# Feed-forward norms: the second token tile's four folds and the last early lo parts queue behind the first tile's normalisation, and the early hi parts form one run

## The chip, the cores and the metric

The kernel runs on one core of a Trainium2 chip. The metric is device time in microseconds of one execution; the time before is the median of three runs. One further execution was profiled, and all rows below are from it. Four engines matter: the tensor engine (PE), the vector engine (VectorE, shown as DVE), the scalar engine (ScalarE, shown as ACT) and the SP queue that issues the weight loads. Each executes its own list of instructions strictly in the order in which they stand, and waits on semaphores for the others.

## The reference, cut to what matters

```python
def _swiglu(x, w1, w3, w2):
    return (silu(x @ w1) * (x @ w3)) @ w2

for l in range(2):                     # x: 256 tokens x 1024
    x = _layernorm(ALPHA * x + 0.5 * _swiglu(x, w1[l,0], w3[l,0], w2[l,0]), g[l,0], b[l,0])
    x = _layernorm(ALPHA * x + Mixer(x), g[l,1], b[l,1])
    x = _layernorm(ALPHA * x + 0.5 * _swiglu(x, w1[l,1], w3[l,1], w2[l,1]), g[l,2], b[l,2])
```

Mixer(x) starts with a projection of x (its `val` section) and ends with `m @ w_out`. There are two layers with three layer norms each: four behind a feed-forward part (the last of them makes the output) and two behind a mixer.

## The kernel before, in words

**Tiles.** The 256 tokens are two token tiles of 128 (t = 0, 1; `xtok_143` and `xtok_144` in the lists below). The 1024 columns are two halves (c or h = 0, 1).

**Weights.** `stream` (L154) loads 128x2048 float32 of weights with one DMA into a buffer `raw` (there are four), ScalarE writes a rounded copy, the hi part (L173), and VectorE the rest, the lo part (L175). Matmuls use (hi, x hi), (lo, x hi), (hi, x lo). Parts named `whi`/`wlo` take slots of a pool of eight; at a transition `gemm_b2` borrows room from another pool for the first six 512-wide pieces, named `lhi`/`llo` here: the early parts (`lent`, L327: both halves of the first load and one half of the second).

**End of a feed-forward part** (`ffn`, from L654). The last product, h @ w2, is made with a seven-product scheme; its products lie in banks S[1] to S[7]. VectorE folds them into x: `ln.more` (L475 to L480) is one 128x512 fold. There are two folds for tile 0 and four for tile 1: `more(1, 0, S[7])` at L667, and those with v, u and S[7] at L674 to L676. Then for each tile and half the held weight pieces give the rest of the product into one more bank (`rows_p`, L681: 24 matmuls), and `ln.part` adds that bank to x (L487) and takes statistics of the half (L492). `ln.finish` (L496) aggregates them (L499), computes the reciprocal square root in eight steps on one column (`rsqrt`, L187 to L193), and normalises two halves (L503). This is called the first (t = 0) or the second (t = 1) normalisation below.

**The way into the next stage.** The tensor engine transposes the normalised halves (`turn`, L547): those of tile 0 stand in its list among the products of tile 1, and those of tile 1 among the first products of the next stage. ScalarE applies gain and bias to a transposed half (`xf`, L553) and writes x hi (L180), VectorE x lo (L181). The next stage begins with `gemm_b2` (L321): tile 0 with all four loads, then tile 1 with the same parts.

**What sets the order.** The tensor engine's list is the order of the code, with `turn` placed by a count of beats. On the other engines a scheduler orders instructions by priority and by when it expects inputs. Two means override it: `soon()` raises the priority of ScalarE's and VectorE's work on the transposes, and `behind(ins)` queues an instruction behind `ins` on that engine. Early hi parts are queued behind `latest[0]`, the last x hi of the stage before. The lo parts have `after` (L328): in the second load the early half has none of its own, so it falls back on `latest[1]`, and the other half is queued behind `norm.ends[0]`, the first normalisation.

Of the kernel before, what the change touches and what calls it, by code (L numbers as in the profile page):

```python
# [16 lines left out]
AF = mybir.ActivationFunctionType  # L17
ALU = mybir.AluOpType
# [23 lines left out]
HC = CH // 2  # L42
# [15 lines left out]
def trunk(ctx, tc, x, xT, w13a, w13b, w2s, w2p, wb, wqk, wa, wbr, wo, gateb, sgug, sgub, sguwT, sgubias, lam, diffg,  # L58
# [88 lines left out]

    latest, added, emptied, silu, turned_by = [None, None], [None], [None], [None], [None]

# [4 lines left out]
    def stream(src, width=CH, sub=HC, lent=(), after=(None, None)):  # L154
# [7 lines left out]
        for o in range(0, width, HC):  # L162
# [7 lines left out]
            for p, (h, w) in zip(range(0, HC, sub), at):  # L170
                r = raw[:, o + p : o + p + sub]
                with behind(latest[0]):
                    A.activation(h, r, AF.Copy)  # L173
                with behind(after[o // HC] or latest[1]):
                    V.tensor_tensor(out=w, in0=r, in1=h.bitcast(F32), op=ALU.subtract)  # L175
# [145 lines left out]
    def gemm_b2(srcs, xh, xl, done, norm=None):  # L321
# [4 lines left out]
        if norm:  # L326
            lent = [(0, 1), (0,), (), ()]  # L327
            after[1:3] = (None, norm.ends[0]), (norm.ends[0], norm.ends[0])  # L328
        ps = [[bank() for _ in range(2)] for _ in range(NT)]
        got = [[None] * 4 for _ in range(2)]  # L330
        for t in range(NT):
            for c in range(2):
# [3 lines left out]
                for m in range(2):  # L336
                    n = 2 * c + m
                    if t == 0:
                        got[m][2 * c : 2 * c + 2] = stream(srcs[m][:, c * CH : (c + 1) * CH], sub=512, lent=lent[n],
                                                           after=after[n])  # L340
                    for i in range(2 * c, 2 * c + 2):
                        rows_b(ps[t][m], t, 2 * i, got[m][i], xh, xl, KT)
            with behind(latest[0] if t == 0 else None):
                done(t, ps[t])
# [221 lines left out]
    def ffn(l, f, i, norm, last=False):  # L566
# [99 lines left out]
        ln.more(0, 0, S[1], ALU.add, ln.scale)  # L666
        ln.more(1, 0, S[7], ALU.subtract, ln.scale)  # L667
        V.tensor_tensor(out=u, in0=u, in1=S[1], op=ALU.add)
        V.tensor_tensor(out=v, in0=S[5], in1=u, op=ALU.subtract)
        ln.more(0, 1, v, ALU.add, ln.scale)  # L670
        for m in range(HELD // 2):
            q = PQ[len(PQ) - HELD + 2 * m :][:2]
            held.update({(k, 1): w for k, w in zip(q, stream(w2p[l, f, len(PQ) - HELD // 2 + m]))})
        ln.more(1, 1, v, ALU.add, ln.scale)  # L674
        ln.more(1, 0, u, ALU.add)
        ln.more(1, 1, S[7], ALU.add)  # L676
        for t in range(NT):
            for c in range(2):
                for ps, o, n in ends[t, c]:
                    for q in PQ[-HELD:]:  # L680
                        rows_p(ps, t, q, held[q, c], hh, hl, o, n, stop=q == PQ[-1])  # L681
                    for o in ((0, 256) if last and (t, c) == (1, 1) else (0,)):
                        ln.part(t, c * 512 + o, ps[:, o : o + 256] if o or last and (t, c) == (1, 1) else ps, 1.0)
            ln.finish(t, ((2, 1.5), (2, 1))[t])
        return ln.close()

# [319 lines left out]
```

## Time and profile before

| | us |
|---|---|
| median of three runs (1225.89 to 1226.11) | 1226.04 |
| the profiled execution | 1224.48 |
| its span, first to last instruction | 1222.7 |
| PE busy | 1209.9 (99%) |
| DVE busy | 954.5 (78%) |
| ACT busy | 813.1 (66%) |

1.78 us of the profiled execution lie around its span. A row of the timeline is: start in us, duration in us (of the whole group where it ends in x2 or more), engine, line, operation, output <- input, shapes, count, and in brackets the idle time of the engine just before it with what ended it. Overlapping durations are normal: a next instruction can begin before the one ahead has ended.

### The profile page before, as it was taken

How to read it: one execution, taken by the hardware profiler on the slowest of the kernel's cores; microseconds unless marked ns; L12 is line 12 of the kernel's file. 1: busy time of each engine (PE TensorE's matmuls, PEld its weight loads, DVE VectorE, ACT ScalarE, POOL GpSimd, SP SyncE). 2: the span in 40 equal slices, each digit the busy share in tenths (PEclk: the TensorE clock that was granted, in tenths of full speed). 3: DMA queues.
4: the chain of work that ended last, by engine and by line, in shares of the span. 5: the costliest groups of instructions: out<-in, count | busy, mean ns of one | idle time of the engine just before them, and what ended most of it. 6: DMA issues, size and time to landing. Idle time of an engine off the chain costs nothing.

```text
span 1222.7 us, 16592 instructions
## 1 busy us (share of the span) xinstructions
PE 1209.9 (99%) x6033; PEld 1018.2 (83%) x6033; DVE 954.5 (78%) x1540; ACT 813.1 (66%) x1328; POOL 88.0 (7%) x184
## 2 busy tenths in 40 slices
PE   9999999999999999999999999999999999999998
PEld 8888878888888888888788888788888888888886
DVE  6658998886587985679985679978856879747797
ACT  7677666679665665775666776666795655667761
POOL 0100000244100000000000000002430000000000
PEclk9999999999999999999999999999999999999999
DMA  8975665654754657675667655756446446577551
GB/s 318 333 245 180 220 225 202 218 168 167 248 172 166 219 181 254 194 202 207 238 192 251 197 175 206 268 189 211 161 171 240 172 163 250 175 238 206 182 202 49
DMA packets 82339, 252.29 MB, mean 206 GB/s; under 512 B 47520, under 2 KB 48592, under 8 KB 55632
## 3 DMA queue, kind: packets, MB, share of 16 engines
q1 hardware_dynamic: 78288, 238.31, 58.0%
q0 software_dynamic: 3536, 12.13, 2.9%
q8 instruction: 47, 0.77, 0.2%
q10 hardware_dynamic: 432, 0.79, 0.2%
q14 instruction: 36, 0.29, 0.1%
HBM read 235.47 MB, written 1.05 MB: 193 GB/s over the span
## 4 chain that ended last, share of the span: by engine, by line
PE 89%; DVE 7%; issue 2%; ACT 1%; DMA 0%; DVEq 0%; ACTq 0%
PE bank L215 34%; PE sbank L215 21%; PE bank L227 17%; PE bank L234 9%; PE sbank L227 2%; PE bank L386 2%; DVE wlo L175 2%; DVE slo L299 1%; PE sbank L736 1%; PE sbank L547 1%; PE sbank L234 1%; DVE llo L175 1%; PE sbank L785 1%; PE sbank L866 1%; DVE raw L310 1%
## 5 line engine op out<-in xcount | busy, mean ns | idle before, releaser
L175 DVE TENSOR_TENSOR wlo<-raw,whi 128x1024 fp32r<-128x1024 f32 (+1 forms) x402 | 441.3, 1116 | 158.5 <-ACT whi L173 118.2
L173 ACT ACTIVATE whi<-raw 128x1024 fp32r<-128x1024 f32 (+1 forms) x402 | 378.7, 966 | 181.3 <-PE bank L215 62.1
L215 PE MATMUL bank<-whi,x 128*128 128x512 f32 x840 | 264.6, 390 | 0.0
L215 PEld LDWEIGHTS bank<-whi,x 128*128 128x128 f32 x840 | 157.7, 188 | 32.6
L215 PE MATMUL bank<-wlo,x 128*128 128x512 f32 x420 | 163.5, 389 | 0.0
L215 PE MATMUL sbank<-whi,x 128*128 128x512 f32 x512 | 158.9, 389 | 0.0
L227 PE MATMUL bank<-x,whi 128*128 128x512 f32 x640 | 158.3, 395 | 0.0
L227 PEld LDWEIGHTS bank<-x,whi 128*128 128x128 f32 x640 | 116.5, 188 | 26.0 <-issue 2.7
L215 PEld LDWEIGHTS sbank<-whi,x 128*128 128x128 f32 x512 | 96.1, 188 | 19.9
L297 ACT ACTIVATE shi<-raw 128x1024 fp32r<-128x1024 f32 (+1 forms) x80 | 73.4, 946 | 51.8 <-DVE raw L312 26.7
L215 PE MATMUL sbank<-wlo,x 128*128 128x512 f32 x256 | 99.6, 389 | 0.0
L299 DVE TENSOR_TENSOR slo<-raw,shi 128x1024 fp32r<-128x1024 f32 (+1 forms) x80 | 85.2, 1087 | 14.4 <-ACT shi L297 13.6
L215 PEld LDWEIGHTS bank<-wlo,x 128*128 128x128 f32 x420 | 78.9, 188 | 16.0
L234 PE MATMUL bank<-x,wlo 128*128 128x256 f32 x640 | 85.8, 285 | 0.0
L234 PEld LDWEIGHTS bank<-x,wlo 128*128 128x128 f32 x640 | 81.5, 191 | 2.3
L553 ACT ACTIVATE xf<-sbank,ln_b,ln_g 128x128 f32<-128x128 f32 x80 | 30.0, 456 | 45.8 <-PE sbank L547 45.8
L235 ACT ACTIVATE r<-bank 128x256 f32<-128x256 f32 x112 | 41.8, 379 | 27.6 <-PE bank L234 27.6
L215 PEld LDWEIGHTS sbank<-wlo,x 128*128 128x128 f32 x256 | 48.0, 188 | 10.1
L215 PE MATMUL sbank<-whi,hhi 128*128 128x512 f32 x144 | 56.3, 391 | 0.0
L215 PE MATMUL sbank<-whi,hlo 128*128 128x512 f32 x144 | 56.1, 389 | 0.0
L215 PE MATMUL sbank<-wlo,hhi 128*128 128x512 f32 x144 | 56.0, 389 | 0.0
L446 POOL DMA_DIRECT2D bc<-in_lng x6 | 3.2, 530 | 712.1 <-DVE bc L445 712.1
(233 smaller groups left out, 1977.0 us busy)
## 6 DMA issues: line engine op xcount, KB each, us to landing
raw<-in_w13b SPq DMA_DIRECT2D x76, 1024.0 KB, 5.4
raw<-in_w2p SPq DMA_DIRECT2D x24, 1024.0 KB, 4.9
raw<-in_wa SPq DMA_DIRECT2D x24, 1024.0 KB, 5.3
raw<-in_w2s SPq DMA_DIRECT2D x20, 1024.0 KB, 4.8
raw<-in_wb SPq DMA_DIRECT2D x16, 1024.0 KB, 4.9
raw<-in_wqk SPq DMA_DIRECT2D x16, 1024.0 KB, 4.8
raw<-in_wbr SPq DMA_DIRECT2D x16, 1024.0 KB, 4.8
raw<-in_w13a SPq DMA_DIRECT2D x8, 1024.0 KB, 4.8
```

What stands on the lines that cost most here:

```text
L173: A.activation(h, r, AF.Copy)
L175: V.tensor_tensor(out=w, in0=r, in1=h.bitcast(F32), op=ALU.subtract)
L215: PE.matmul(ps, xx, w, start=start and n == 0, stop=stop and n == 2)
L227: PE.matmul(b[-1], hi[:, k * P : (k + 1) * P], xc(k), start=k == 0, stop=False)
L234: PE.matmul(b[n][:, :T], lo[:, k * P : (k + 1) * P], xc(k)[:, :T], start=False, stop=k == KT - 1)
L235: emptied[0] = A.activation(r[:, s], b[n][:, T:], AF.Copy, scale=scale).ins
L297: A.activation(h, r, AF.Copy)
L299: V.tensor_tensor(out=w, in0=r, in1=h.bitcast(F32), op=ALU.subtract)
L310: V.tensor_tensor(out=raw[:, :1024], in0=raw[:, :1024], in1=raw[:, 512:1536], op=ALU.add)
L386: PE.matmul(ps[t][m], x[:, j, o + t * P : o + (t + 1) * P], y, start=k0 + j == 0 and o == 0 and y is hi, stop=k0 + j == KT - 1 and y is lo)
L547: PE.transpose(b[:, k * P : (k + 1) * P], self.y[t][:, h * 512 + k * P : h * 512 + (k + 1) * P], ident)
L553: A.activation(xf[:, s], b[:, s], AF.Identity, scale=self.gT[:, f], bias=self.bT[:, f])
```

## The change

- `ffn`: the four folds of tile 1 are no longer issued with those of tile 0; they stand behind `ln.finish(0)`, queued behind the second half of the first normalisation (`ln.ends[0]`). In the last feed-forward part there is no such instruction (`ends[0]` stays None), and only their place in the code moves.
- `gemm_b2`: `after[1:3]` now queues both halves of the second load, and so the last two early lo parts, behind the first normalisation. This is so behind the mixers' norms too.
- `stream`: a hi part that isn't early is queued behind the last early hi part given so far (`early[0]`) instead of behind `latest[0]`; the early ones stand as one run.

```diff
-    latest, added, emptied, silu, turned_by = [None, None], [None], [None], [None], [None]
+    latest, added, emptied, silu, turned_by, early = [None, None], [None], [None], [None], [None], [None]
...
-                with behind(latest[0]):
-                    A.activation(h, r, AF.Copy)
+                with behind(latest[0] if o // HC in lent else early[0] or latest[0]):
+                    copied = A.activation(h, r, AF.Copy)
+                if o // HC in lent:
+                    early[0] = copied.ins
...
-            after[1:3] = (None, norm.ends[0]), (norm.ends[0], norm.ends[0])
+            after[1:3] = [(norm.ends[0], norm.ends[0])] * 2
...
+            early[0] = None
             with behind(latest[0] if t == 0 else None):
                 done(t, ps[t])
...
         ln.more(0, 0, S[1], ALU.add, ln.scale)
-        ln.more(1, 0, S[7], ALU.subtract, ln.scale)
...
-        ln.more(1, 1, v, ALU.add, ln.scale)
-        ln.more(1, 0, u, ALU.add)
-        ln.more(1, 1, S[7], ALU.add)
...
             ln.finish(t, ((2, 1.5), (2, 1))[t])
+            if t == 0:
+                with behind(ln.ends[0]):
+                    ln.more(1, 0, S[7], ALU.subtract, ln.scale)
+                    ln.more(1, 0, u, ALU.add)
+                    ln.more(1, 1, v, ALU.add, ln.scale)
+                    ln.more(1, 1, S[7], ALU.add)
```

In the changed file the lines stand a little lower: L175 becomes L177, L181 L183, L480 L483, L487 L490, L492 L495, L503 L506, L547 L550, L553 L556. The lists of the tensor engine, GpSimd and SP are the same as before, row for row. VectorE's and ScalarE's differ at the norms: in the same way behind the first three feed-forward parts, in another behind the two mixers, and in the last feed-forward part only tile 1's folds move, between tile 0's two sums.

VectorE ahead of the first normalisation of the first norm (L503), before: three of tile 1's folds, the first sum of tile 0 (`bank_1213`) and what follows.

```order
L480 SCALAR_TENSOR_TENSOR xtok_144<-xtok_144,v_1492 128x512
L478 TENSOR_TENSOR xtok_144<-xtok_144,u_1491 128x512
L478 TENSOR_TENSOR xtok_144<-xtok_144,sbank_1210 128x512
L487 TENSOR_TENSOR xtok_143<-xtok_143,bank_1213 128x512
L175 TENSOR_TENSOR llo_1720<-raw_1716,lhi_1718 128x512
L492 BN_STATS st_1199<-xtok_143 128x6
L487 TENSOR_TENSOR xtok_143<-xtok_143,sbank_1209 128x512
```

The same engine in the change, from the first normalisation (L506) on.

```order
L506 TENSOR_SCALAR xtok_143<-xtok_143,mv_1590,nwy_1605 128x512 x2
L483 SCALAR_TENSOR_TENSOR xtok_144<-xtok_144,sbank_1210 128x512
L483 SCALAR_TENSOR_TENSOR xtok_144<-xtok_144,v_1492 128x512
L481 TENSOR_TENSOR xtok_144<-xtok_144,u_1491 128x512
L481 TENSOR_TENSOR xtok_144<-xtok_144,sbank_1210 128x512
L490 TENSOR_TENSOR xtok_144<-xtok_144,sbank_1211 128x512
L177 TENSOR_TENSOR llo_1750<-raw_1746,lhi_1748 128x512
L495 BN_STATS st_1200<-xtok_144 128x6
L177 TENSOR_TENSOR llo_1751<-raw_1746,lhi_1749 128x512
L183 TENSOR_TENSOR x_1207<-xf_1651,x_1207 128x4x128
```

Eight rows that stood ahead of the first normalisation now stand behind it: the four folds, the two early lo parts `llo_1750` and `llo_1751`, and tile 1's first sum (`sbank_1211`) with its statistics, which need the folds.

VectorE ahead of the second normalisation of the same norm, before: from the reciprocal square root on, with x lo of the second half (`x_1208`).

```order
L181 TENSOR_TENSOR x_1208<-xf_1681,x_1208 128x4x128
L193 TENSOR_SCALAR nwy_1701<-nwa_1700,nwy_1697 128x1
L175 TENSOR_TENSOR wlo_1815<-raw_1812,whi_1814 128x512
L192 TENSOR_SCALAR nwa_1704<-nwy_1701,ve_1692 128x1
L175 TENSOR_TENSOR wlo_1815<-raw_1812,whi_1814 128x512
L193 TENSOR_SCALAR nwy_1705<-nwa_1704,nwy_1701 128x1
L175 TENSOR_TENSOR wlo_1821<-raw_1812,whi_1820 128x512
L503 TENSOR_SCALAR xtok_144<-xtok_144,mv_1690,nwy_1705 128x512 x2
L175 TENSOR_TENSOR wlo_1821<-raw_1812,whi_1820 128x512
```

The same place in the change.

```order
L177 TENSOR_TENSOR wlo_1783<-raw_1774,whi_1782 128x512
L194 TENSOR_SCALAR nwa_1696<-yi_1693,ve_1692 128x1
L177 TENSOR_TENSOR wlo_1815<-raw_1812,whi_1814 128x512
L195 TENSOR_SCALAR nwy_1697<-nwa_1696,yi_1693 128x1
L177 TENSOR_TENSOR wlo_1815<-raw_1812,whi_1814 128x512
L194 TENSOR_SCALAR nwa_1700<-nwy_1697,ve_1692 128x1
L177 TENSOR_TENSOR wlo_1821<-raw_1812,whi_1820 128x512
L195 TENSOR_SCALAR nwy_1701<-nwa_1700,nwy_1697 128x1
L177 TENSOR_TENSOR wlo_1821<-raw_1812,whi_1820 128x512
L194 TENSOR_SCALAR nwa_1704<-nwy_1701,ve_1692 128x1
L195 TENSOR_SCALAR nwy_1705<-nwa_1704,nwy_1701 128x1
L506 TENSOR_SCALAR xtok_144<-xtok_144,mv_1690,nwy_1705 128x512 x2
```

All four pieces of the last load (`wlo_1815`, `wlo_1821`) now stand ahead of the second normalisation; before, the last of them stood behind it.

ScalarE at the same norm, before: its hi parts end (`whi_1820`) ahead of tile 0's first transposed half (`xf_1651`).

```order
L173 ACTIVATE lhi_1749<-raw_1746 128x512
L173 ACTIVATE whi_1782<-raw_1774 128x512 x2
L173 ACTIVATE whi_1814<-raw_1812 128x512 x2
L173 ACTIVATE whi_1820<-raw_1812 128x512 x2
L553 ACTIVATE xf_1651<-sbank_1646,ln_b,ln_g 128x128 x4
```

ScalarE in the change, from the fifth early hi part on.

```order
L173 ACTIVATE lhi_1748<-raw_1746 128x512
L556 ACTIVATE xf_1651<-sbank_1646,ln_b,ln_g 128x128 x4
L173 ACTIVATE lhi_1749<-raw_1746 128x512
L182 ACTIVATE x_1207<-xf_1651 128x4x128
L173 ACTIVATE whi_1756<-raw_1746 128x512 x2
L173 ACTIVATE whi_1776<-raw_1774 128x512 x2
L173 ACTIVATE whi_1782<-raw_1774 128x512
L556 ACTIVATE xf_1681<-sbank_1676,ln_b,ln_g 128x128 x4
```

The run of early hi parts is broken by the first transposed half: the sixth (`lhi_1749`) and all hi parts behind it now stand behind `xf_1651`, and so behind the tensor engine's first transposes.

## The prediction

> **What bounds the kernel now.** I read the page's busy times first: the tensor engine works nearly all the time, so only its few idle places can be won.
>
> ```profile
> PE 1209.9 (99%) x6033; PEld 1018.2 (83%) x6033; DVE 954.5 (78%) x1540; ACT 813.1 (66%) x1328; POOL 88.0 (7%) x184
> ```
>
> Then who waits for whom, on the tensor engine alone (total us, times, longest). The first two entries are the transposes at line 547: three waits, 6.1 us of the 12.8 us of the span in which the engine is not busy.
>
> ```profile
> PE sbank L547 <- DVE xtok L503: 4.1, 2, 2.2
> PE sbank L547 <- issue: 2.0, 1, 2.0
> ```
>
> The timeline shows the three places: tile 0's first transposes behind the first three feed-forward parts, each with the last matmul ahead of it.
>
> ```profile
> 177.54 0.39 PE L215 MATMUL sbank<-whi,hlo 128*128 128x512 f32 x1
> 179.88 0.63 PE L547 MATMUL sbank<-ident,xtok 128*128 128x128 f32 x4 [1.95 <-issue]
> ```
> ```profile
> 603.28 0.39 PE L215 MATMUL sbank<-whi,hlo 128*128 128x512 f32 x1
> 605.85 0.66 PE L547 MATMUL sbank<-ident,xtok 128*128 128x128 f32 x4 [2.17 <-DVE xtok L503]
> ```
> ```profile
> 783.97 0.39 PE L215 MATMUL sbank<-whi,hlo 128*128 128x512 f32 x1
> 786.27 0.66 PE L547 MATMUL sbank<-ident,xtok 128*128 128x128 f32 x4 [1.91 <-DVE xtok L503]
> ```
>
> Where nothing waits, transposes start 0.23 us after the matmul ahead. Tile 0's second half shows it in the first norm, and the next rows of interest are tile 1's first half there.
>
> ```profile
> 184.22 0.39 PE L215 MATMUL sbank<-whi,hlo 128*128 128x512 f32 x1
> 184.45 0.60 PE L547 MATMUL sbank<-ident,xtok 128*128 128x128 f32 x4
> ```
> ```profile
> 191.74 0.60 PE L547 MATMUL sbank<-ident,xtok 128*128 128x128 f32 x4
> ```
>
> So the stalls really cost 2.34 - 0.23 = 2.11, 2.57 - 0.23 = 2.34 and 2.30 - 0.23 = 2.07 us, together 6.5 us. That is all this change can take away at the first transposes.
>
> Whom does the tensor engine wait for? Busy times over the stretch from the first fold to tile 1's transposes (length, then PE, weight load, DVE, ACT and POOL busy with their counts, granted clock, DMA share, GB/s):
>
> ```profile
> 161.00:191.00 30.00, 28.05 (x128) 23.01 (x127) 29.50 (x60) 15.35 (x29) 0.00 (x0) 1.00 0.68 245
> ```
>
> VectorE, 78% busy over the kernel, is 98% busy here. In this stretch it is the bound, and the stall is its backlog. This row decides the forecast: a new order gives VectorE no room, it only chooses which of its results comes late.
>
> **First term: the first normalisation.** Consecutive 128x512 operations on VectorE start 0.60 us apart:
>
> ```profile
> 168.59 0.68 DVE L480 SCALAR_TENSOR_TENSOR xtok<-xtok,v 128x512 f32<-128x512 f32 x1
> 169.20 0.69 DVE L478 TENSOR_TENSOR xtok<-xtok,u 128x512 f32<-128x512 f32 x1
> 169.80 0.68 DVE L478 TENSOR_TENSOR xtok<-xtok,sbank 128x512 f32<-128x512 f32 x1
> 170.40 0.68 DVE L487 TENSOR_TENSOR xtok<-xtok,bank 128x512 f32<-128x512 f32 x1
> ```
>
> Without the four folds the sum at 170.40 starts at 170.40 - 4 x 0.60 = 168.0. In the new order five operations follow (an early lo part, the statistics, three early lo parts), so tile 0's second sum starts at 168.0 + 6 x 0.60 = 171.6. Its last matmul has ended by then, at 170.74 + 0.39 = 171.13:
>
> ```profile
> 170.74 0.39 PE L215 MATMUL sbank<-whi,hlo 128*128 128x512 f32 x1
> ```
>
> An operation that needs the one just ahead starts 0.72 us after it (the same pair for tile 1):
>
> ```profile
> 184.65 0.69 DVE L487 TENSOR_TENSOR xtok<-xtok,sbank 128x512 f32<-128x512 f32 x1
> 185.37 0.69 DVE L492 BATCH_NORM_STATS2 st<-xtok 128x6 f32<-128x512 f32 x1
> ```
>
> So statistics at 172.3 and the aggregate at 173.05. The small steps then stand alone, as they already do behind a mixer, where the aggregate is followed by L503 after 2.29 us:
>
> ```profile
> 420.80 0.20 DVE L499 BATCH_NORM_AGGREGATE mv<-st 128x2 f32<-128x12 f32 x1
> ...
> 423.09 1.00 DVE L503 TENSOR_SCALAR xtok<-xtok,mv,nwy 128x512 f32<-128x512 f32 x2
> ```
>
> The first normalisation starts at 173.05 + 2.29 = 175.3. Transposes that wait for L503 start 0.60 us after it, as the second ones behind the mixer do:
>
> ```profile
> 436.39 1.00 DVE L503 TENSOR_SCALAR xtok<-xtok,mv,nwy 128x512 f32<-128x512 f32 x2
> ```
> ```profile
> 436.64 0.39 PE L215 MATMUL bank<-whi,x 128*128 128x512 f32 x1
> 436.99 0.66 PE L547 MATMUL sbank<-ident,xtok 128*128 128x128 f32 x4
> ```
>
> They could start at 175.9, and the tensor engine wants them at 177.54 + 0.23 = 177.77. The stall goes, with 1.8 us to spare: **minus 2.11 us** here, minus 6.5 over three norms.
>
> **Second term: the second normalisation.** What is late next? Behind both halves of L503 (0.91 us, the distance of the two rows below) VectorE runs the four folds, tile 1's first sum, an early lo part and the statistics: 175.3 + 0.91 + 7 x 0.60 = 180.4. Next is the last early lo part. Its hi part now stands on ScalarE behind the first transposed half:
>
> ```profile
> 180.55 1.50 ACT L553 ACTIVATE xf<-sbank,ln_b,ln_g 128x128 f32<-128x128 f32 x4 [1.14 <-PE sbank L547]
> 182.08 0.63 ACT L180 ACTIVATE x<-xf 128x512 fp32r<-128x512 f32 x1
> ```
>
> ScalarE starts 0.67 us after the transposes (179.88 to 180.55) and takes 1.50 us, and I take 0.6 for a 512-wide hi part, from the copy of that width: 177.77 + 0.67 + 1.50 + 0.6 = 180.5. VectorE waits about 0.1 us, behind that wait stands everything to the second normalisation, and the two sides meet almost exactly.
>
> From 180.5: this lo part, x lo of the first half and two lo parts, 4 x 0.60, so tile 1's second sum starts at 182.9. Its bank is ready: it let the sum start at 184.65 before, and now comes 2.11 earlier. Up to L503 stand eleven such operations, 6.6 us (the sum, the statistics, x lo of the second half, eight lo parts), with nine small steps between. Wrapped in large ones, a small step costs 0.07, 0.12 or 0.19:
>
> ```profile
> 175.01 0.15 DVE L188 TENSOR_SCALAR yi<-ve 128x1 int32<-128x1 int32 x1
> 175.08 0.68 DVE L175 TENSOR_TENSOR llo<-raw,lhi 128x512 fp32r<-128x512 f32 x1
> ```
> ```profile
> 188.07 0.21 DVE L193 TENSOR_SCALAR nwy<-nwa,nwy 128x1 f32<-128x1 f32 x1
> 188.19 0.68 DVE L175 TENSOR_TENSOR wlo<-raw,whi 128x512 fp32r<-128x512 f32 x1
> 188.79 0.27 DVE L192 TENSOR_SCALAR nwa<-nwy,ve 128x1 f32<-128x1 f32 x1
> 188.98 0.68 DVE L175 TENSOR_TENSOR wlo<-raw,whi 128x512 fp32r<-128x512 f32 x1
> ```
>
> Two at 0.07, two at 0.12, two at 0.19, the aggregate about 0.12, and the last two, which stand alone, 0.54 (their durations and 0.03 for each wait): 1.42 us. The second normalisation starts at 182.9 + 6.6 + 1.42 = 190.9. A second way gives the same: VectorE is full before and after, and ahead of this row stands what stood there before plus one lo part, the row at 191.21.
>
> ```profile
> 190.30 0.99 DVE L503 TENSOR_SCALAR xtok<-xtok,mv,nwy 128x512 f32<-128x512 f32 x2
> 191.21 0.68 DVE L175 TENSOR_TENSOR wlo<-raw,whi 128x512 fp32r<-128x512 f32 x1
> ```
>
> 190.30 + 0.60 = 190.9. Tile 1's transposes then start at 191.5. Without a stall the tensor engine would be there at 191.74 - 2.11 = 189.63. It waits 1.9 us for the second normalisation instead of 2.1 for the first, and is ahead by 191.74 - 191.5 = 0.2 us. The other two norms have the same rows; I count **minus 0.2 three times**.
>
> Bounds: were all nine small steps at 0.07, the cheapest row, the gain would be 0.8 us larger at each place; at the 2.29 us of the steps that stand alone, 0.9 smaller. So from minus 1.0 to plus 0.7 each; I keep the middle, since the wrapped rows are from this very chain. [...]
>
> **Smaller terms.** Behind the two mixers only the two early lo parts move, and the first transposes don't wait there. The second wait 436.99 - 436.64 - 0.23 = 0.12 us; with a lo part less ahead of the first normalisation that chain should start sooner and the wait go: minus 0.1 twice, bounds 0.3 either way. In the last feed-forward part VectorE has 2.6 us to spare ahead of its tail, so its folds cost nothing wherever they stand:
>
> ```profile
> 1214.45 0.42 DVE L487 TENSOR_TENSOR xtok<-xtok,sbank 128x256 f32<-128x256 f32 x1 [2.56 <-PE sbank L215]
> ```
>
> The bank S[7] is held until the last fold ends at 178.7. The only transposes that take its place, tile 0's second, come at 184.45 - 2.11 = 182.3: nothing. No moved row issues a DMA, but loads of the stage behind wait for `raw` buffers. Four go out as buffers come free, each lands some 4.8 us later, and ScalarE first reads one of them at 198.62:
>
> ```profile
> 175.79 16.50 SPq L160 DMA_DIRECT2D raw<-in_wqk  x4
> ```
> ```profile
> raw<-in_wqk SPq DMA_DIRECT2D x16, 1024.0 KB, 4.8
> ```
> ```profile
> 198.62 2.01 ACT L173 ACTIVATE whi<-raw 128x1024 fp32r<-128x1024 f32 x2
> ```
>
> By the account above the third buffer's last lo part now ends near 182.9 + 7 x 0.60 + 0.3 = 187.4, so that load lands by 192.2: the 6 us to its reader hide it; uncovered, its delay would cost some 3 us at a norm.
>
> **Sum.** 3 x (-0.2) + 2 x (-0.1) = -0.8 us: 1224.48 becomes 1223.7. The profiled execution was 1.56 us under the median, so the forecast for the median is 1226.04 - 0.8 = **1225.2 us**. A difference under 0.2%, 2.45 us, can't be told from none.
>
> **Rivals.** *The gain is kept whole.* The stall at the first transposes is real and its cause stands right there, which speaks for it. Then the second normalisation would have to start by 189.63 - 0.60 = 189.0, 1.9 us sooner than VectorE's list allows at 98% busy. Time: 1226.04 - 6.5 - 0.2 = 1219.3. [...] Chance 0.08.
>
> *ScalarE's new place binds.* The last early hi part and all hi parts behind it now wait for the first transposes. From 180.5 on, each 0.1 us that the transposes are late is late at the second normalisation too, and so at the tensor engine, three times. If the first transposes gained nothing and stayed at 179.88, the second normalisation would come at 190.9 + 2.1 = 193.0 and its transposes at 193.6, 1.9 us behind before: 3 x 1.9 - 0.2 = plus 5.5, 1231.5. It passes 0.2% from some 1.1 us a place. Against it stands the 1.8 us that the first transposes have to spare. Chance 0.06.
>
> **How the numbers follow.** The forecast has the remaining 0.86. Its bounds are 3 x (-1.0) - 0.2 = -3.2 and 3 x 0.7 - 0.2 = +1.9: 1222.8 to 1227.9, and I take these as the range, which leaves out only the rivals. Of the 0.86 some 0.05 lie below minus 2.45 us (the cheap small steps) and 0.03 above it (a wait of ScalarE's that I mis-sized): faster 0.13, same 0.78, slower 0.09.
>
> **What would show it.** Right: at all three norms tile 0's first transposes follow the matmul ahead without idle time, L506 starts near 175.3, and a new idle time of 1.5 to 2.3 us stands ahead of tile 1's first transposes, ended by the second normalisation; VectorE is still 98% busy there. Wrong on the first term: a wait left at tile 0's transposes. Wrong on the second: tile 1's transposes without idle time (the gain kept), or VectorE idle for ScalarE ahead of the last early lo part (the second rival).

## The result and the profile after

| | before | after |
|---|---|---|
| median, 13 runs each (us) | 1226.04 (1224.23 to 1228.04) | 1223.33 (1223.05 to 1223.84) |
| the profiled execution | 1224.48 | 1223.12 |
| its span | 1222.7 | 1221.4 |

The ratio is 0.9979, with a 95% interval of 0.997 to 0.9987. The forecast was minus 0.8 us; the medians differ by 2.7, the profiled executions by 1.36. The 1.35 us between these two differences are the open question, and the experiments begin with it.

First the waits of the tensor engine after the change (total us, times, longest). The three waits at the transposes are still there, 5.0 us in all where they were 6.1.

```profile
PE sbank L550 <- DVE xtok L506: 5.0, 3, 1.7
```

The timeline shows that they have moved. In the first norm, tile 0's transposes follow 0.23 us behind the matmul ahead, and tile 1's wait.

```profile
177.42 0.39 PE L217 MATMUL sbank<-whi,hlo 128*128 128x512 f32 x1
177.65 0.60 PE L550 MATMUL sbank<-ident,xtok 128*128 128x128 f32 x4
...
189.28 0.39 PE L217 MATMUL bank<-whi,x 128*128 128x512 f32 x1
191.33 0.66 PE L550 MATMUL sbank<-ident,xtok 128*128 128x128 f32 x4 [1.65 <-DVE xtok L506]
```

It is the same in the other two norms, here tile 1's transposes of the third:

```profile
794.89 0.39 PE L217 MATMUL bank<-whi,x 128*128 128x512 f32 x1
796.94 0.66 PE L550 MATMUL sbank<-ident,xtok 128*128 128x128 f32 x4 [1.66 <-DVE xtok L506]
```

From the start of the matmul to the start of the transposes it takes 2.05 us (the *pitch* of the stall below), 1.82 more than the usual 0.23. VectorE's rows say why: the first normalisation, the last early lo part, tile 1's second sum, the aggregate and the second normalisation.

```profile
175.19 1.00 DVE L506 TENSOR_SCALAR xtok<-xtok,mv,nwy 128x512 f32<-128x512 f32 x2
...
179.71 0.68 DVE L495 BATCH_NORM_STATS2 st<-xtok 128x6 f32<-128x512 f32 x1
180.34 0.69 DVE L177 TENSOR_TENSOR llo<-raw,lhi 128x512 fp32r<-128x512 f32 x1
...
182.76 0.68 DVE L490 TENSOR_TENSOR xtok<-xtok,sbank 128x512 f32<-128x512 f32 x1
...
185.15 0.20 DVE L502 BATCH_NORM_AGGREGATE mv<-st 128x2 f32<-128x12 f32 x1
...
190.73 1.00 DVE L506 TENSOR_SCALAR xtok<-xtok,mv,nwy 128x512 f32<-128x512 f32 x2
```

Before, the first normalisation stood here:

```profile
179.24 1.00 DVE L503 TENSOR_SCALAR xtok<-xtok,mv,nwy 128x512 f32<-128x512 f32 x2
```

So the first normalisation is 4.05 us earlier, the second (190.30 before) 0.43 later, and VectorE is as full as it was (length of the stretch, then PE, weight load, DVE, ACT and POOL busy with counts, granted clock, DMA share, GB/s):

```profile
161.00:191.00 30.00, 28.67 (x131) 23.36 (x129) 29.54 (x59) 14.85 (x29) 0.00 (x0) 1.00 0.66 236
```

The tensor engine's list is the same in both kernels and both traces hold its 6033 matmuls, so the n-th matmul of one can be set against the n-th of the other. Counted so, the transposes of tile 0 gain 2.11, 2.33 and 2.07 us at the three norms, and those of tile 1 give back 1.81, 1.81 and 1.82. That leaves 0.30, 0.52 and 0.25, together 1.07 of the 1.36 us; the rest are mostly two steps of 0.1 to 0.2 us, at the start of the kernel and inside the second mixer (at 882 us), and 0.03 at each mixer's norm.

### The profile page after: what moved, and what is told of

Same layout as the page of the kernel before. It is cut to its first block, busy times and chain, and to the rows that moved or that the text cites. A ratio compares the mean times of both kernels' runs of the same rounds, so it can differ in the third digit from the quotient of the medians.

```text
span 1221.4 us, 16592 instructions
## 1 busy us (share of the span) xinstructions
PE 1210.1 (99%) x6033; PEld 1018.4 (83%) x6033; DVE 955.1 (78%) x1540; ACT 811.5 (66%) x1328; POOL 89.0 (7%) x184
## 3 DMA queue, kind: packets, MB, share of 16 engines
HBM read 235.47 MB, written 1.05 MB: 194 GB/s over the span
## 4 chain that ended last, share of the span: by engine, by line
PE 82%; DVE 13%; issue 3%; ACT 2%; DMA 0%; DVEq 0%; ACTq 0%
PE bank L217 30%; PE sbank L217 17%; PE bank L229 17%; PE bank L236 9%; DVE wlo L177 3%; PE sbank L229 2%; DVE slo L301 2%; PE bank L389 2%; PE sbank L741 1%; DVE llo L177 1%; DVE raw L312 1%; ACT shi L299 1%; DVE xtok L490 1%; DVE st L495 1%; DVE raw L314 1%
## 5 line engine op out<-in xcount | busy, mean ns | idle before, releaser
L177 DVE TENSOR_TENSOR wlo<-raw,whi 128x1024 fp32r<-128x1024 f32 (+1 forms) x402 | 441.1, 1113 | 159.2 <-ACT whi L173 119.1
L556 ACT ACTIVATE xf<-sbank,ln_b,ln_g 128x128 f32<-128x128 f32 x80 | 30.1, 458 | 63.2 <-PE sbank L550 63.2
```

The costliest lines, as they stand in the source:

```text
L556: A.activation(xf[:, s], b[:, s], AF.Identity, scale=self.gT[:, f], bias=self.bT[:, f])
```

## Experiments

### Where the other 1.35 us come from

Line numbers shift by a few from kernel to kernel with each edit; the operations stay the same.

**The kernel before, once more, unchanged.**

> The kernel before, unchanged, profiled a second time. Its 13 runs lie at 1225.81 to 1226.70 us in ten cases, at 1224.23 and 1224.48 in two and at 1228.04 in one; the profiled one was 1224.48, so the pair of profiled executions differs by 1.36 us and the medians by 2.7. Theory A (a step at one place): a typical execution loses some 1.5 us at one place where the first profile lost nothing, and a profile of 1225.8 to 1226.7 shows one more wait there, which the changed kernel does not have. Theory B (scatter): such a profile is longer by many small amounts all over the span, and the place of the change accounts for 1.1 us only. If the profiled execution is again near 1224.4, this run can't tell them apart. The three stalls at tile 0's first transposes are there in any case, 2.3 to 2.6 us each from the matmul ahead.

Measured: 1225.9 us in the median (11 runs, 1224.19 to 1228.04). The profiled execution was one of the short ones again, 1224.27, and its matmuls agree with the first profile's to 0.2 us, so it can't tell the two theories apart. But with the 33 runs of the kernel before beside it there are 44 runs now, and they stand in three groups: 16 at 1223.88 to 1224.66 us, 25 at 1225.72 to 1226.81 and 3 at 1227.56 to 1228.04. (Of the 54 other runs of this kernel, with the result and beside the later experiments, 8, 40 and 5 fall near these groups, and one, at 1339.17 us and a mean clock of 0.851, far outside.) The mean granted clock of the tensor engine goes with them: 1.0 in the first group, 0.998 or 0.999 in the second (one run 1.0), 0.997 in the third. The changed kernel's 13 runs all lie within 0.8 us, at 0.999 or 1.0.

**Only the hi parts' new rule.**

```diff
...
-                with behind(latest[0]):
-                    A.activation(h, r, AF.Copy)
+                with behind(latest[0] if o // HC in lent else early[0] or latest[0]):
+                    copied = A.activation(h, r, AF.Copy)
+                if o // HC in lent:
+                    early[0] = copied.ins
...
+            early[0] = None
```

> The kernel before with only the hi parts' new rule (those that aren't early queue behind the last early one). VectorE's list is that of before at the norms. The theory on record: nothing changes at the first three norms, the three stalls of 2.1 to 2.3 us stay, 0.0 us within 0.3. Rival (ScalarE's order matters by itself, through when raw buffers come free or when VectorE finds its inputs): a change of the first or the second normalisation of more than 0.3 us at the norms, and of the whole time by 1 us or more.

Measured: 1226.19 us (11 runs, 1224.03 to 1227.61; ratio to before 1.0008, 0.9999 to 1.0017). The three stalls are as before. This part is worth nothing, as the theory on record had it. The profiled execution, though, was one of the second group (1225.59 us), and it shows what such a run has. Matched with the first profile of before, it is ahead by 0.39 us at the transposes of the third norm, and then falls back by 1.63 us in steps of mostly 0.2 us, one for each matmul:

```profile
783.64 0.39 PE L217 MATMUL sbank<-whi,hlo 128*128 128x512 f32 x1
785.88 0.88 PE L550 MATMUL sbank<-ident,xtok 128*128 128x128 f32 x4 [1.85 <-DVE xtok L506]
...
786.99 0.63 PE L217 MATMUL sbank<-wlo,hhi 128*128 128x512 f32 x1
787.42 0.63 PE L217 MATMUL sbank<-whi,hlo 128*128 128x512 f32 x1
787.84 0.63 PE L217 MATMUL sbank<-whi,hhi 128*128 128x512 f32 x1
...
789.81 0.39 PE L217 MATMUL sbank<-whi,hlo 128*128 128x512 f32 x1
790.04 0.40 PE L217 MATMUL sbank<-whi,hhi 128*128 128x512 f32 x1
```

The products start 0.43 us apart instead of 0.23, and the windows give the granted clock (the third number from the end) as about half for it:

```profile
784.00:786.00 2.00, 0.15 (x2) 0.12 (x2) 1.89 (x6) 0.63 (x1) 0.00 (x0) 1.00 0.77 324
786.00:788.00 2.00, 2.00 (x8) 1.71 (x9) 2.00 (x4) 1.20 (x4) 0.00 (x0) 0.54 0.02 4
788.00:790.00 2.00, 2.00 (x7) 1.56 (x6) 2.00 (x5) 1.34 (x3) 0.00 (x0) 0.61 0.58 172
790.00:794.00 4.00, 4.00 (x21) 3.28 (x20) 2.10 (x5) 1.27 (x4) 0.00 (x0) 1.00 1.01 422
```

So a stall has a second price. Behind it the clock can fall to half, in a part of the executions, and here it did so for 2 x 0.46 / 0.5 + 2 x 0.39 / 0.5 = 3.4 us, with half taken as 0.5 (the granted clock in the tail of the change's trace is 0.50, from 1220.2 to 1221.3 us). From here on this was the theory for the 1.35 us: the first profile of before happened to have no such fall, the median execution has one. One fall lowers the mean clock of a run by 0.5 x 3.4 / 1224 = 0.0014. A mean of 0.999 alone does not show one, since the change's profile has that mean from half clock in its last 1.3 us and none at the norms; and the run of the second group at a mean of 1.0 (1226.22 us) can't have had one and stays unexplained.

### The parts of the change by themselves

**Only the four folds moved** (lo parts and hi parts as before).

```diff
-        ln.more(1, 0, S[7], ALU.subtract, ln.scale)
...
-        ln.more(1, 1, v, ALU.add, ln.scale)
-        ln.more(1, 0, u, ALU.add)
-        ln.more(1, 1, S[7], ALU.add)
...
+            if t == 0:
+                with behind(ln.ends[0]):
+                    ln.more(1, 0, S[7], ALU.subtract, ln.scale)
+                    ln.more(1, 0, u, ALU.add)
+                    ln.more(1, 1, v, ALU.add, ln.scale)
+                    ln.more(1, 1, S[7], ALU.add)
```

> The kernel before with only tile 1's four folds moved behind the first normalisation; the early lo parts and all hi parts stay where they were. The theory on record (VectorE is full, and what stands ahead of the second normalisation decides): the first normalisation comes at 176.4 (last statistics of tile 0 at 173.4, the steps behind them stand alone), in time for the transposes at 177.8, so the first stall goes at all three norms; ahead of the second normalisation stand the same operations as in the change, so it starts near 190.9 and tile 1's transposes get a new idle time of some 1.8 us: minus 0.3 us a norm, minus 0.8 in all by the profile, and in the medians what the change has, minus 2.7, if the rest of that comes from somewhere else. First rival (ScalarE's place of the sixth early hi part sets the second normalisation): here the hi parts stand ahead of the first transposed half, so the second normalisation would come sooner than in the change and the new idle time be clearly under 1.6 us. Second rival (the gain at the first transposes is kept, and the early lo parts eat it up in the change): minus 6 us.

Measured: 1224.38 us (11 runs, 1223.49 to 1226.23). The first stall is gone and the new one stands at tile 1:

```profile
178.00 0.39 PE L215 MATMUL sbank<-whi,hlo 128*128 128x512 f32 x1
178.23 0.60 PE L548 MATMUL sbank<-ident,xtok 128*128 128x128 f32 x4
...
189.87 0.39 PE L215 MATMUL bank<-whi,x 128*128 128x512 f32 x1
192.02 0.66 PE L548 MATMUL sbank<-ident,xtok 128*128 128x128 f32 x4 [1.76 <-DVE xtok L504]
```
```profile
615.54 0.39 PE L215 MATMUL bank<-whi,x 128*128 128x512 f32 x1
617.93 0.66 PE L548 MATMUL sbank<-ident,xtok 128*128 128x128 f32 x4 [2.00 <-DVE xtok L504]
```

The pitch is 2.15, 2.39 and 2.13 us, a little longer than the change's 2.05. The last hi part that the early lo parts need stands far ahead here, and the stall is not shorter for it: ScalarE's place does not set the second normalisation, and the first rival falls. The second falls too (it asked for minus 6 us). The median is 1.05 us over the change's, where none was expected: matched matmul by matmul, the longer stalls make 0.6 of it, so that against the first profile of before the three norms give minus 0.4 us and not 0.8; what the rest of the 1.05 is was not settled. And two of the 11 runs, 1225.57 and 1226.23 at clocks of 0.998 and 0.999, stand apart as before's second group does.

**Only the two early lo parts moved.**

```diff
-            after[1:3] = (None, norm.ends[0]), (norm.ends[0], norm.ends[0])
+            after[1:3] = [(norm.ends[0], norm.ends[0])] * 2
```

> The kernel before with only the last two early lo parts queued behind the first normalisation; folds and hi parts as before. The theory on record: the first normalisation starts at some 177.85 instead of 179.24 (two lo parts and one statistics less ahead of it, more of the small steps alone), so that of the 2.11 us of real stall some 0.7 us are left; ahead of the second normalisation stands one lo part more than before, so it starts at about 190.9 and tile 1's transposes wait some 1.2 us: minus 0.2 us a norm, minus 0.7 in all, no difference to the change. Rival (each microsecond won at the first transposes is kept): minus 1.4 us a norm, minus 4.3.

Measured: 1223.32 us (11 runs, 1223.03 to 1223.76), the same as the whole change, from one line. It does so in another way: a short stall at each place.

```profile
177.97 0.39 PE L215 MATMUL sbank<-whi,hlo 128*128 128x512 f32 x1
178.90 0.63 PE L547 MATMUL sbank<-ident,xtok 128*128 128x128 f32 x4 [0.53 <-issue]
...
190.53 0.39 PE L215 MATMUL bank<-whi,x 128*128 128x512 f32 x1
191.71 0.65 PE L547 MATMUL sbank<-ident,xtok 128*128 128x128 f32 x4 [0.80 <-DVE xtok L503]
```

0.93 - 0.23 = 0.70 us are left of the first stall, as expected, and 1.18 - 0.23 = 0.95 us are lost at the second. Their sum, 1.65, is near the 1.82 us of the change; by matched matmuls the three norms give minus 1.2 us against before, 0.5 more than expected. Wherever the first stall is cut, the second normalisation comes out at nearly the same time, and the tensor engine meets it there: counted from the same matmul ahead of the first place, at 190.55 us here and 190.83 with the folds alone, against the change's 190.73. The rival (minus 4.3 us) falls.

### The budget ahead of the second normalisation

If the number of VectorE operations ahead of the second normalisation is what holds the gain back, taking some away must release it, and adding some must cost. The last load's four lo pieces are the ones to move: they are read last.

**All four behind the second normalisation**, on top of the change.

```diff
-                    after[3] = [norm.xlo.get((0, 1))] * 2
+                    after[3] = [norm.ends[1]] * 2
```

> The changed kernel with all four lo pieces of the last load queued behind the second normalisation (in the change all four stand ahead of it; the tensor engine reads the first of them only at 193.44 us). Theory on record (the number of VectorE operations ahead of the second normalisation sets tile 1's transposes): four operations of 0.60 us less ahead of it, and some 0.5 us lost because the last six small steps stand alone: L506 at about 188.9 instead of 190.73, transposes at 189.5, where the tensor engine wants them at 189.28 + 0.23 = 189.51. The idle time of 1.82 us beyond the usual pitch goes at all three norms: minus 5.0 to 5.4 us against the change, 1218.0 to 1218.4 in the median, with runs as close together as the change's. Rival 1 (ScalarE's sixth early hi part, behind the first transposed half, sets the second normalisation): L506 stays within 0.5 us of 190.7 and VectorE shows idle time ahead of the last early lo part or behind it: minus 1.5 us or less. Rival 2 (what is put behind the normalisation is late in its turn): a new wait of the tensor engine at the products with the last lo pieces eats up more than 1 us a norm.

Measured: 1217.6 us (5 runs, 1217.38 to 1218.02), minus 5.7 against the change and 0.4 below the range that was expected; the ratio to before is 0.9935 (0.9921 to 0.9948). This beats both kernels. There is no idle time at either place any more:

```profile
189.78 0.39 PE L217 MATMUL bank<-whi,x 128*128 128x512 f32 x1
190.01 0.60 PE L550 MATMUL sbank<-ident,xtok 128*128 128x128 f32 x4
```

On VectorE the normalisation comes sooner by the operations that left, and these follow it; in this trace the stretch begins 0.49 us later than in the change's, so 189.33 stands against 190.73 + 0.49 = 191.22, 1.89 us sooner (four operations of 0.60 less 0.5 for small steps that now stand alone, as expected). The tensor engine works through the whole stretch.

```profile
189.33 1.00 DVE L506 TENSOR_SCALAR xtok<-xtok,mv,nwy 128x512 f32<-128x512 f32 x2
190.25 2.49 DVE L177 TENSOR_TENSOR wlo<-raw,whi 128x512 fp32r<-128x512 f32 x4
```
```profile
161.00:191.00 30.00, 30.00 (x140) 24.77 (x139) 29.40 (x59) 15.72 (x30) 0.00 (x0) 1.00 0.65 236
```

VectorE is as busy as ever (29.40 of 30 us). Nothing was taken from it; only results that nobody waits for were put behind the one that is waited for. Matched with the change, tile 1's transposes gain 1.81, 1.81 and 1.82 us, those behind the mixers another 0.14 and 0.13, and no later wait takes it back: the second rival of this run falls as well.

**Only two of the four.**

```diff
-                    after[3] = [norm.xlo.get((0, 1))] * 2
+                    after[3] = [norm.xlo.get((0, 1)), norm.ends[1]]
```

> As the run before this one, but only two of the four pieces stand behind the second normalisation. Theory on record: two operations of 0.60 us less, some 0.25 us lost by small steps that stand alone: L506 at about 189.8, transposes at 190.35, an idle time of 0.85 us beyond the usual pitch instead of 1.82: minus 2.9 us against the change, 1220.4. It lies between the change and the run before this one, in the proportion of what is left ahead of the second normalisation. Rival 1 (ScalarE sets it): no gain.

Measured: 1220.1 us (5 runs, 1219.77 to 1220.22), minus 3.2. The stall is 1.10 - 0.23 = 0.87 us; 0.85 was expected.

```profile
189.22 0.39 PE L217 MATMUL bank<-whi,x 128*128 128x512 f32 x1
190.32 0.66 PE L550 MATMUL sbank<-ident,xtok 128*128 128x128 f32 x4 [0.71 <-DVE xtok L506]
```

**The same four pieces on the kernel before** (the edit is that of the first of these runs).

> The kernel before, and only the four lo pieces of the last load behind the second normalisation. Theory on record: the stall at tile 0's first transposes stays (2.1 to 2.3 us a norm), and tile 1's transposes don't wait in the kernel before, so nothing is won: within 0.5 us of before, with before's three groups of times (near 1224.2, 1226.0, 1227.7). That the same edit is worth 5 us on the changed kernel and nothing here is what the theory needs. Rival (late lo pieces help by themselves): a gain of 2 us or more here too.

Measured: 1225.73 us (11 runs, 1223.91 to 1227.90; ratio 0.9999, 0.999 to 1.0007): nothing. The second normalisation comes 1.5 us sooner (188.78 against 190.30), and nobody waits for it, since the tensor engine is late from the first stall. The edit that is worth 5.7 us behind the change is worth none ahead of it. Its profiled execution (1225.41 us) shows the half clock again, this time from the end of the second norm's stall of 2.56 us on, with granted clocks of 0.59 and 0.55:

```profile
605.00:607.00 2.00, 1.42 (x6) 1.32 (x7) 2.00 (x5) 0.26 (x1) 0.00 (x0) 0.59 0.37 156
607.00:609.00 2.00, 2.00 (x7) 1.57 (x6) 1.45 (x4) 1.87 (x5) 0.00 (x0) 0.55 0.56 94
```

**One operation more ahead of the second normalisation**, on top of the change: one lo part is written twice with the same values.

```diff
-                    V.tensor_tensor(out=w, in0=r, in1=h.bitcast(F32), op=ALU.subtract)
+                    for _ in range(2 if twice and o == p == 0 else 1):
+                        V.tensor_tensor(out=w, in0=r, in1=h.bitcast(F32), op=ALU.subtract)
...
-                                                           after=after[n])
+                                                           after=after[n], twice=bool(norm) and n == 2 and norm.ffn)
...
```

> The changed kernel with one 128x512 lo part made twice ahead of the second normalisation of the first three norms (same values, written again), so that the new idle time of the tensor engine is longer by one VectorE operation, 0.60 us: from 2.05 us between the starts of matmul and transposes to 2.65. By VectorE's list alone: plus 0.6 us at each norm, plus 1.8 us, all runs between 1224.9 and 1225.7. Second theory, formed from the run with only the hi parts changed (behind a stall of 2.24 us seven products stood 0.43 us apart instead of 0.23, at a granted clock of 0.54 to 0.61, and that execution was 1.2 us longer): a stall of 2.2 us and more lets the tensor engine's clock fall to half for some 3 us in a part of the executions, which costs 1.2 to 2 us each time, and stalls of 2.05 us don't. Then the groups of before come back: some runs near 1225.1, others near 1226.8 and 1228.4, the median 1226 or more, and the longer runs have the lower mean clock.

Measured: 1227.86 us (11 runs), in two groups: three runs at 1225.38 to 1225.40 with a mean clock of 0.999, eight at 1227.56 to 1228.14 with 0.996 or 0.997. The profiled one is of the first group. Its stall has a pitch of 2.53 us, 0.48 longer than the change's (0.60 for the operation, less 0.12 for one small step more that stands beside a large one), and its clock is 1.0 behind all three.

```profile
190.04 0.39 PE L218 MATMUL bank<-whi,x 128*128 128x512 f32 x1
192.57 0.66 PE L551 MATMUL sbank<-ident,xtok 128*128 128x128 f32 x4 [2.14 <-DVE xtok L507]
```

By the list alone all runs would be near 1223.3 + 3 x 0.48 = 1224.8, and eight are some 3 us above that. Groups are back, as the clock theory asked, but not its three: runs with one fall, near 1226.8, are missing.

**The same kernel, profiled again.**

> The kernel with one more VectorE operation, profiled once more. Its 11 runs fell into two groups, 1225.38 to 1225.40 us and 1227.56 to 1228.14, and the first profile, at 1225.40, shows full clock behind all three stalls. If the clock is the cause of the second group, a profile of 1227.5 to 1228.2 shows stretches of half clock behind two of the three stalls (2.4 us at some 1.2 each), or one that is twice as long, and nothing else that differs from the first profile by more than 0.3 us. If the cause is another one, the clock is 1.0 behind all stalls and the 2.4 us lie elsewhere. A profile of 1225.4 again tells nothing (about 3 in 11).

Measured: 1224.84 us at a mean clock of 0.999, by its time once more a run without a fall. This run decided nothing; what the second group looks like inside was not seen.

**Two operations more** (the same edit with `range(3 ...)`).

> The changed kernel with the same lo part made three times ahead of the second normalisation (two operations of 0.60 us more than the change, at three norms): the stall between the starts of matmul and transposes becomes 2.05 + 1.2 = 3.25 us. By VectorE's list alone: 1223.3 + 3 x 1.2 = 1226.9 us in all runs, at a mean clock of 0.999 to 1.0. By the clock theory the longer stall lets the clock fall more often, behind two or all three stalls, at 1.2 to 1.3 us each: 1229.3 to 1230.8 in the median, a mean clock of 0.996 or 0.997, and the profile, if it is one of those, shows products 0.43 us apart instead of 0.23 for some 3 us behind the stalls and nowhere else.

Measured: 1228.9 us (6 runs: 1227.53, 1227.67, 1227.90 at a clock of 0.999; 1229.89 at 0.997; 1230.94 and 1230.99 at 0.995). The pitch is 3.0 us, not 3.25, so the list alone gives 1223.3 + 3 x 0.95 = 1226.2, and no run is there. The profiled execution (1227.67) has one fall, at the first norm, where products start 0.43 us apart from 193.49 to 196.05 us and 0.23 again from 196.40 on. Behind the stalls of the other two they are 0.23 apart, as at full clock:

```profile
189.48 0.39 PE L218 MATMUL bank<-whi,x 128*128 128x512 f32 x1
192.49 0.78 PE L551 MATMUL sbank<-ident,xtok 128*128 128x128 f32 x4 [2.62 <-DVE xtok L507]
192.92 0.78 PE L218 MATMUL bank<-whi,x 128*128 128x512 f32 x1
193.49 0.63 PE L218 MATMUL bank<-wlo,x 128*128 128x512 f32 x1
```
```profile
617.44 0.39 PE L218 MATMUL bank<-whi,x 128*128 128x512 f32 x1
620.43 0.66 PE L551 MATMUL sbank<-ident,xtok 128*128 128x128 f32 x4 [2.60 <-DVE xtok L507]
620.85 0.48 PE L218 MATMUL bank<-whi,x 128*128 128x512 f32 x1
621.16 0.40 PE L218 MATMUL bank<-wlo,x 128*128 128x512 f32 x1
```

Matched with the change, it loses 0.96 us to the stall and 1.6 to the clock at the first norm, and 0.95 at each of the others. With 1.5 us a fall the groups are one, two and three of them: 1227.7, 1229.2, 1230.7. The median is a little below the range that was expected.

### Is it a question of which operations are moved?

**Folds and late pieces, without the early lo parts and the hi rule.**

> The kernel before with the four folds behind the first normalisation and the four late lo pieces behind the second; the early lo parts and the hi parts as before. Theory on record: the two places are a budget of VectorE operations each, and it does not matter which ones are moved. The first stall is gone with the folds alone (measured), the second needs four operations less ahead of the second normalisation, which this has too: no idle time at either place, 1217.6 us as with all parts of the change (1217.4 to 1218.0). Rival (the early lo parts and the hi parts behind them are needed for it, since with them ahead of the first normalisation the first transposes come late): 1219 us or more, with idle time at tile 0's transposes.

Measured: 1218.18 us (5 runs, 1217.66 to 1218.79; ratio to before 0.9934, 0.9922 to 0.9947). The median is 0.2 us above the expected range and well under the rival's 1219. Its profiled execution is as long as that of the run with all parts to 0.05 us, but it was 0.54 us ahead when it reached the first norm and lost nearly all of that again: 0.30 us of it at tile 1's transposes of the second norm, the only one of the six places with a pitch clearly over the usual 0.23.

```profile
612.73 0.39 PE L215 MATMUL bank<-whi,x 128*128 128x512 f32 x1
613.26 0.66 PE L548 MATMUL sbank<-ident,xtok 128*128 128x128 f32 x4
```

So the second place is nearly clear with these parts, and not quite at every norm. Whether that makes the 0.6 us between the medians, with five runs each, is not settled.

**Early lo parts and late pieces, folds as before.**

> The kernel before with the two early lo parts behind the first normalisation and the four late lo pieces behind the second; folds as before, ahead of the first. Theory on record: the first stall is only shortened, to the 0.70, 0.94 and 0.65 us that the early lo parts alone left, together 2.3; the second place has room: 1217.6 + 2.3 = 1219.9 us. So the folds, whose move is worth nothing beside the early lo parts in the change, are worth 2.3 us once the second place has room. Rival (the folds' move never mattered): 1217.6.

Measured: 1219.89 us (5 runs, 1219.84 to 1220.08), as expected to 0.01. What is left is the rest of the first stall:

```profile
PE sbank L547 <- DVE xtok L503: 1.3, 2, 0.8
PE sbank L547 <- issue: 0.5, 1, 0.5
```

So the move of the folds (with the hi rule), which adds nothing in the change to what the early lo parts alone reach, is worth 1219.89 - 1217.6 = 2.3 us once the second place has room.

### Stalls and the clock

The runs that stand above their kernel's lowest group, against the pitch of its stalls at the three norms:

| kernel | pitch of the stalls (us) | runs | of them above |
|---|---|---|---|
| two late pieces | 1.10, 1.10, 1.10 | 5 | 0 |
| early lo parts alone | up to 1.21 | 11 | 0 |
| the change | 2.05, 2.04, 2.05 | 13 | 0 |
| folds alone | 2.15, 2.39, 2.13 | 11 | 2 |
| hi rule alone | 2.30, 2.52, 2.24 | 11 | 10 |
| before (44 runs), and late pieces on it (11) | 2.34, 2.57, 2.30 | 55 | 37 |
| one operation more | 2.53, 2.52, 2.52 | 12 | 8 |
| two operations more | 3.01, 2.99, 2.99 | 6 | 6 (against 1226.2) |

The traces say more about when a fall comes. The clock records of before and of the change show a granted clock of 1.0 for 1218.558 and 1215.145 us on end, 357 and 356 times 3.413 us, from 4.39 and 4.95 us behind the start on. The falls that windows show lasted 3.40 us (hi rule alone) and 3.44 us (late pieces on the kernel before). Counted in steps of 3.413 us from these points, which for the profiles with falls is an estimate, the step ahead of the fall holds 1.85 us of idle time of the tensor engine with the hi rule alone (784.03 to 785.88), about 1.96 of the 2.17 with the late pieces on the kernel before (603.41 to 605.37) and, by its rows, all of the 2.62 with two operations more. In the trace of before the three stalls, idle for 1.95, 2.17 and 1.91 us, are each split over two steps, with 1.41, 1.47 and 1.69 us in the larger part, and none brings a fall. A step with 1.87 us (603.38 to 605.25 in the run with the hi rule alone, counted back from its fall at 786.15) brings none either. So the 2.17 us at the second norm brought a fall where 1.96 of them lay in one step and none where 1.47 did: the same stall can bring a fall in one execution and none in another. The stalls of the change are idle for 1.65 and 1.66 us, less than the 1.69 in one step that brought no fall, wherever a step begins; those of before, idle for 1.91 to 2.17, are longer than the 1.85 that brought one.

## Why the prediction was right, and where it was not

**The first term** came as worked out. The first normalisation was computed for 175.3 and stands at 175.19, in a stretch that began 0.14 us earlier; the stalls gave 2.11, 2.33 and 2.07 us where 2.11, 2.34 and 2.07 were counted.

**The second term** came out as well: the second normalisation at 190.9, measured 190.73, with the same 0.14. From tile 1's second sum to it 6.6 + 1.42 = 8.02 us were counted and 190.73 - 182.76 = 7.97 are there. So the wrapped small steps cost what their rows said.

**ScalarE's new place** was to cost 0.1 us at the last early lo part. It costs 0.03 (179.71 + 0.60 = 180.31, and the row stands at 180.34), and the run with the folds alone shows that the stall is there without it. **The mixers** were to give 0.1 each; the matched matmuls show 0.03 each.

**The sum** was minus 0.8 for the profiled pair, which gave 1.07 at the norms and 1.36 in all. The second norm makes most of the difference: its first stall was the longest, 2.34 us by the prediction's own count, and what is given back is the same at all three (1.8 where 1.9 was counted), so 0.2 three times was too little there.

**The step that failed** is the one from the profiled execution to the median: "The profiled execution was 1.56 us under the median, so the forecast for the median is 1226.04 - 0.8". That took the 1.56 us for a constant offset of the profiled run. The groups of times say that it is not one. They point to the price of a clock fall at one of the three stalls, which by their times 28 of the 44 runs of before have; the profiled one had none. The change has stalls of 2.05 us in place of those of 2.30 to 2.57, and at that length no run fell. Against the 16 runs of before in the shortest group (median 1224.3) the change's 1223.33 are minus 0.97, about the sum; the other 1.7 are, by this account, the falls. With them the difference passes the 0.2% bound, to minus 0.22%. That the measured median lies in the forecast's range all the same is owed to the width of the range: the larger part of the difference is a term that the sum did not have. The cause of the falls is shown in so far as three profiles have them, each at the end of a stall or directly behind it, and longer stalls bring more; that the *median* of before is short of exactly this is inferred from the mean clocks of its runs, since neither of its own two profiles caught one.

**The rivals.** The gain was not kept whole, for the reason given: VectorE's list has no room. How much it would have been worth is now measured: with four operations out of the way the time is 1217.6, which is the 1224.3 of before's runs at full clock less the 6.5 us of the stalls and some 0.2. ScalarE's new place did not bind.

## What to carry to other kernels

When an engine is full over a stretch, moving its work from ahead of one waited-for result puts it ahead of the next: list all results in the stretch that others wait for, and move what nobody waits for soon behind the last of them, or both moves measure as nothing (here 0 for the late pieces alone, about 1 us at full clock for the change, 6.7 for the two). And look at the spread of the runs before taking the profiled execution for the median one: here the groups of times went with an event that some executions had (three profiles show it, 1.5 to 1.6 us lost each time), and none of the change's 13 runs stands apart.

## What the hardware showed that was not expected

A stall of the tensor engine of 2.24, 2.56 and 3.01 us (start of the last matmul to start of the transposes) was followed, in three profiled executions, by a stretch in which 128x512 products stood 0.43 us apart instead of 0.23, with 1.5 to 1.6 us lost each time. In two of them the windows give the granted clock there, 0.54 and 0.61, and 0.59 and 0.55, which makes 3.40 and 3.44 us at half clock. Stalls of the same length in the same and other executions were followed by full clock (2.30 and 2.52 us with the hi rule alone, 2.99 twice with two operations more), and of the kernels with stalls of 2.05 us or less no run stands apart from the others. What sets the clock was not shown. The times at half clock lie near the 3.413 us of which the full clock lasted 357 and 356 in the traces of before and of the change. Counted in steps of that length, falls came behind 1.85, about 1.96 and 2.62 us of idle time in one step, and none behind 1.87 in one execution or behind 1.69 and less in before's. By these figures a limit, if there is one, lies near 1.7 to 1.9 us (an estimate); a kernel made to meet it was not run. Open is also why the kernel with one operation more had runs 2.4 us longer and none 1.5 longer.
